# Norm statistics of a two-block fp32 transformer kernel: plain sums and row broadcasts by transposes and a row sum, in place of fp32 products with ones and with the identity

## The chip, the cores and the metric

The kernel runs on one NeuronCore of a Trainium2 chip. The metric is the time of one execution on the device in microseconds (us); the lower, the better. The kernel before takes 892.62 us, the median of 3 runs (891.92 to 893.26).

## The reference

Two transformer blocks run one after the other on one sequence of 256 tokens with 1024 features, all in fp32. The first block has a sliding-window attention layer with sinks and a block attention layer. The second has two layers, each a hybrid mixer (dilated attention beside a chunked state-space scan) and a gated feed-forward. What the change touches are the norms:

```python
def rmsnorm(x, g):
    y = x * lax.rsqrt(jnp.mean(x * x, axis=-1, keepdims=True) + NORM_EPS)
    return y * g

def first_block(x, ...):
    h = x
    for i in range(DEPTH):                 # 2 layers: phases a, ao and b, bo
        hn = rmsnorm(h, norm_g[i])
        ...                                # q, k, v, z; rope; attention
        h = h + (o * jax.nn.silu(z)) @ w_out[i]
    return rmsnorm(h, final_g)

def second_block(x, ...):
    for layer in range(DEPTH):             # phases m0, mo0, f0, fo0 and m1, mo1, f1, fo1
        h = h + hybrid_mixer(rmsnorm_2(h, norm_mix[layer]), ...)
        h = h + swiglu(rmsnorm_2(h, norm_ffn[layer]), ...)
    return rmsnorm_2(h, final_norm)
```

Inside the hybrid mixer the scan's output is normalised once more, in two groups of 512 features. That makes six norms over 1024 features on the way (phases a, b, m0, f0, m1, f1; the one of m0 has two sums, because the final norm of the first block and the first norm of the second block are taken together), four group norms, and the last norm of all.

## The kernel before

Features lie on the 128 partitions and tokens along the free axis, so that a tile is 128 features by 256 tokens. Every dense product is made of three f32r products (high part by high, high by low, low by high), which are matmuls of 128x128 weights with 128x256 moving columns. ScalarE (ACT) rounds an operand or a weight tile to its high part (names `hi`, `r`, `x`), VectorE (DVE) makes the low part (`lo`). Weights come in by DMA on SyncE's queue (L1451).

The whole program is written out in advance, in the order of an expected timeline. The class `Build` keeps a clock for each engine. `cost` (L219) holds the expected time of an instruction and `account` (L247) adds it to the clocks. The planner `run_plan` (L471) goes through a fixed list of dense products and issues one slot of them as soon as its operands are expected. Everything else (norms, rotary embedding, softmax, scan) runs in side chains, Python generators whose next step `step_sides` (L298) issues once its operands are expected to be there. So the side work stands between dense products, at places that depend on every expected time. A side chain takes one of the 8 PSUM banks by `take` (L282) and returns it by `give` (L287). There are limits by kind: 2 banks at most for kind "tr", which the norms share with the transposes of the attention and of the scan. On each engine the instructions then run strictly in the order of the program.

All instructions pass through one helper, so the profile puts them all on line L78, and they are told apart by tile names: the phase, two underscores, the tile. `a__sm` is the tile `sm` of phase a; matmul outputs are called `p`.

The norm (`norm`, L650) runs as a side chain with these steps:

- `squares` (L891) adds up x squared over the feature tiles, and `columns` (L579) adds the two halves on VectorE into `sm` [128 features, 256 tokens].
- TensorE multiplies each half of `sm` with a column of ones, in native fp32. The result is a column of sums, tokens on partitions, in PSUM: `p<-ones,sm`, 128x1 twice.
- VectorE divides and adds epsilon (`s<-p`, 128x2), and GpSimd (POOL) takes the power -1/2.
- `rows` (L622) turns the column into rows on all partitions: a native fp32 product of the column, broadcast along the free axis, with the identity, twice (`p<-cst,s`; `cst` holds the identity). VectorE copies the row out of PSUM (`row`, and `rowh`, its half).

The dense products of a phase start before its norm is done: the norm's scale per token is applied when a finished unit leaves PSUM (`q`, `k`, `v` tables, `zh`, `u`, `up`). A phase has one norm, and m0 calls `columns` with two sums and `rows` twice: in all 11 pairs of products with ones and 11 pairs with the identity. `scan_out` (L1240) calls `norm` for the group norms in phases mo0 and mo1. The last norm of the program and the sums of the scan's time steps do not use these functions.

Two chains of other work matter below. The attention issues, for a pair of heads, the score products (`p<-rope,rope`, TensorE), a masked minimum on VectorE (`sm<-p,cst`, shown as CUSTOM_DVE), the exponential on ScalarE (`pe`), the scaling on VectorE (`pe<-pe,s`), three transposes per head on TensorE (`p<-cst,pe`), a copy (`pt`) and the product with the values (`p<-pt,vk`). The last attention outputs of a phase are the last operands of the output projection (phases ao, bo, mo0, mo1). In the scan, ScalarE makes decay masks (`m`), and TensorE multiplies them (`p<-m,xg`).

Of the kernel before, what the change touches and what calls it, by code (L numbers as in the profile page):

```python
# [16 lines left out]
OP = mybir.AluOpType  # L17
# [11 lines left out]
# column offsets of the packed per-feature vectors  # L29
# [14 lines left out]
# column offsets of the constants (they depend on shapes alone)  # L44
# [20 lines left out]
class Engine:  # L65
    """Passes instructions on and notes how long they are expected to take."""
# [24 lines left out]
class Chain:  # L91
    """A generator of steps; a step is issued once what it waits for is expected to be there."""
# [7 lines left out]
class Timed(dict):  # L100
    """Results with the times at which they are expected."""
# [11 lines left out]
class Build:  # L113
    """Emits the program in the order of an expected timeline: the dense products keep the tensor engine
    busy, and the steps of the side chains are issued between them as their operands come up."""
# [84 lines left out]
    def drop(self, n=1):  # L200
        """n pages have had their last use issued."""
        self.live -= n
# [16 lines left out]
    def cost(self, eng, op, args, kw):  # L219
# [21 lines left out]
        if eng == "POOL":  # L241
            return 650.0
        if op in ("tensor_copy", "tensor_scalar") and not psum:
            return 68.0 + 0.52 * n + 93.0 * cols
# [20 lines left out]
    def calm(self, ns):  # L265
        """Hold new side work back while the vector or scalar engine has much to do."""
        while max(self.clk["DVE"], self.clk["ACT"]) > self.clk["PE"] + ns:
            yield "poll"

    def bank_at(self, kind):  # L270
        """When a PSUM bank can be had, or None."""
        if self.used[kind] >= self.CAPS[kind] or not self.banks:
            return None
        if kind == "mm" and self.used["mm"] >= 3 and len(self.banks) < 4:
            return None
        return min(self.banks)
# [21 lines left out]
    def step_sides(self):  # L298
        """Issue every step that is due; the least time at which another will be."""
# [25 lines left out]
    def seg(self, key, w, unit, k0, k1, kt, xkey, done, mode="T", page=False):  # L325
        """Plan the contraction tiles k0..k1 of one unit of 256 columns."""
# [7 lines left out]
    def feed_dma(self):  # L334
        """Load the next segment."""
# [18 lines left out]
    def feed(self):  # L354
        """Issue loads and splits ahead of the products."""
# [3 lines left out]
        while self.cast_i < self.dma_i and self.cast_slot < self.slot + self.LEAD:  # L359
# [15 lines left out]
            if s["mode"] == "dt":  # L375
                # both parts of the 16 columns side by side
                both = hi[:, :, 0:32]
                raw, hi, lo = raw[:, :, 0:16], both[:, :, 0:16], both[:, :, 16:32]
            else:
                lo = self.fp.tile([P, n, S], F32R, tag="f", name=self.name("lo"))  # L380
# [20 lines left out]
    def slot_ready(self):  # L401
        """When the next slot of the dense products can start, if that is known."""
# [121 lines left out]
    def rotary_tables(self):  # L524
        """Tables of the second block from the positions."""
# [39 lines left out]
    def split_scaled(self, h, off, u, key, g=None):  # L565
        """Parts of h * g for one unit of two feature tiles."""
# [12 lines left out]
    def columns(self, accs, ns):  # L579
        """Sums of squares [128, 2, 256] -> 1/rms per token in columns [128, 2]; a second sum is of the  # L580
        values once normalised by the first."""
# [9 lines left out]
        ps = self.bank("tr", (P, 4))  # L591
        for j, sm in enumerate(sms):
            for b in range(2):
                nc.tensor.matmul(ps[:, 2 * j + b:2 * j + b + 1], sm[:, b * P:(b + 1) * P], self.ones[:, 0:1],
                                 start=True, stop=True, skip_group_check=True)
            self.drop()
        yield 1
        cols = []
# [6 lines left out]
        self.give("tr")  # L605
# [16 lines left out]
    def rows(self, rc, key, half=True):  # L622
        """Columns per token -> [128, 256] rows on every partition (and their half)."""
# [3 lines left out]
        for b in range(2):  # L627
            nc.tensor.matmul(pr[:, b * P:(b + 1) * P], rc[:, b:b + 1].to_broadcast([P, P]), self.ident,
                             start=True, stop=True)
# [16 lines left out]
    def keep(self, key, n=1):  # L646
        """n pages that live as long as the phase."""
# [12 lines left out]
    def spare(self, ns):  # L660
        """Whether the scalar engine is free ns earlier than the vector engine."""
# [3 lines left out]
    def scaled(self, out, src, scale):  # L665
        """out = src * scale (a column per partition) on the engine that is free first."""
# [20 lines left out]
    def rope(self, ps, nt, tab, mask, key, give=True):  # L687
        """nt tiles of PSUM [128, nt, 256] rotated."""
# [18 lines left out]
    def v_tokens(self, ps, row, key):  # L707
        """[128 channels, 256 tokens] -> [128 tokens, 2 blocks, 128 channels]"""
# [33 lines left out]
    def gate_unit(self, key, u):  # L742
        """silu of the normalised columns."""
# [15 lines left out]
    def scores(self, q, k, mask, sinks, key, last):  # L759
        """Scores of two heads; they take different rows of the array, side by side."""  # L760
# [16 lines left out]
    def head(self, sc, mask, sink, key):  # L777
        """Probabilities of one head, keys on partitions:
        [keys 0..127 x queries 0..255 | keys 128..255 x queries 128..255]"""
# [38 lines left out]
    def attention(self, key, units, kname, vcols, mask, sinks, finish):  # L818
        """Heads in pairs of tiles; finish(u, po) takes the two tiles of a unit from PSUM."""
# [55 lines left out]
    def out_unit(self, key, u, hkey, hnext, scale):  # L875
        """h += o @ w for one unit, with the parts of the next norm's input."""
# [36 lines left out]
    def plan_out(self, key, w, kt, cuts, hkey, hnext, scale):  # L913
        """The contraction tiles that come up late are left to later parts of the units."""
# [7 lines left out]
    def plan_in(self, lst):  # L922
        """Units of 8 contraction tiles; the first two leave the tiles that come last to the end."""
# [142 lines left out]
    def dt_unit(self, l):  # L1066
        """dt and a = dt * a_neg, [128 tokens, 2 blocks, 16 heads] each."""
        def done(ps):
# [49 lines left out]
            # cumulated a per block of tokens (negated), and from a token to the end of the first block  # L1118
# [17 lines left out]
            # the sums per head on the partitions, as three parts of bf16 that add up to them  # L1136
# [20 lines left out]
    def cb_chain(self, l):  # L1157
        """B C^T with the earlier tokens on partitions, per group: first block x all tokens, second x second."""
# [16 lines left out]
    def decay(self, l, u, c):  # L1175
        """M^T = exp(sum of a from a token to a later one) * B C^T of four heads, earlier tokens on partitions;
        c is the block of the later tokens."""
# [34 lines left out]
    def state_inputs(self, l, u):  # L1212
        """xs of four heads with tokens on partitions times dt; xs itself times d_skip."""
# [26 lines left out]
    def scan_out(self, l, u):  # L1240
        """Outputs of four heads, gated, and the group norm once its two units are there."""
# [49 lines left out]
    def plan_m(self, l):  # L1291
# [36 lines left out]
        def residual():  # L1328
            # the first block's output: h * final_g / rms
# [48 lines left out]
    def last_unit(self, t0, n):  # L1378
        """The last residual for feature tiles t0..t0+n-1: sums of squares per token, and the tiles times the
        final gain with tokens on partitions; with the last of them the result."""  # L1380
# [68 lines left out]
    def load(self, out, src, n):  # L1449
        """A load of n bytes per partition; its tile's results come up when it has landed."""  # L1450
# [87 lines left out]
def _units(w, cols):  # L1538
    """[K, N] -> [units, 128, K / 128, 256], columns in the given order."""
# [5 lines left out]
def _feat(v):  # L1545
    """[..., n * 128] -> [128, rows * n]"""
# [107 lines left out]
```

## Time and profile before

| what | us |
|---|---|
| median of 3 runs | 892.62 |
| span of the profiled execution | 889.3 |
| TensorE (PE) busy | 872.1 (98%) |
| VectorE (DVE) busy | 702.4 (79%) |
| ScalarE (ACT) busy | 527.0 (59%) |
| GpSimd (POOL) busy | 12.8 (1%) |
| DMA, mean rate | 160 GB/s |

The profile is one execution, whose span runs from its first to its last recorded instruction. The median lies 3.3 us above that span. The span is cut into stretches by the phases: the chain that ended last gives phase b's dense products from 108.14 us, bo 180.45, m0 210.39, mo0 some 316, f0 356.31, fo0 483.91, m1 547.27, mo1 649.48, f1 687.33 us. A row of the timeline has a start and a duration; matmuls overlap in the pipeline, so that what a matmul costs is read from the start of the next one and not from its duration. A native fp32 product is recorded as two instructions, so that a pair shows as "x4".

### The profile page before, as it was taken

The numbers are of one execution on the slowest core, as the hardware profiler recorded it, in microseconds if no ns is written. First come the engines' busy times: TensorE is split into PE (matmuls) and PEld (weight loads), VectorE is DVE, ScalarE is ACT, GpSimd is POOL, SyncE is SP. The second block draws the span as 40 slices with busy tenths as digits, with TensorE's granted clock in tenths as the row PEclk, the third lists the DMA queues.
The fourth block names the chain that finished last, engine by engine and source line by source line (L and its number), as shares of the span: only waits on it lengthen the run. The fifth ranks groups of instructions, "written<-read, shape, count | busy, mean of one in ns | idle before, by whom it ended". The sixth has DMA issues, their size and how long they took to land.

```text
span 889.3 us, 18454 instructions
## 1 busy us (share of the span) xinstructions
PE 872.1 (98%) x7318; PEld 841.8 (95%) x7318; DVE 702.4 (79%) x1542; ACT 527.0 (59%) x1217; POOL 12.8 (1%) x30
## 2 busy tenths in 40 slices
PE   6999999999999999999999999999999999999996
PEld 6987999889998889999999999999999999999996
DVE  5999889998899998998667547888988898667331
ACT  6378753677778875665345446668656675444321
POOL 0000000000000000000000000000000000000000
PEclk9999999999999999999999999999999999999998
DMA  8522773035542146767444637520047687545501
GB/s 298 205 86 72 236 262 125 26 114 179 186 152 98 37 131 208 278 241 280 153 157 146 220 132 245 185 73 25 1 134 225 244 282 258 186 132 171 173 1 48
DMA packets 30390, 142.39 MB, mean 160 GB/s; under 512 B 5344, under 2 KB 6880, under 8 KB 18400
## 3 DMA queue, kind: packets, MB, share of 16 engines
q1 hardware_dynamic: 30304, 141.22, 46.8%
q8 instruction: 57, 0.93, 0.4%
q14 instruction: 29, 0.24, 0.1%
HBM read 140.15 MB, written 1.05 MB: 159 GB/s over the span
## 4 chain that ended last, share of the span: by engine, by line
PE 68%; issue 21%; DVE 5%; ACT 3%; DMA 2%; SPq 1%; POOL 0%; POOLq 0%; DVEq 0%
PE m__p L78 21%; PE f__p L78 15%; PE mo__p L78 9%; PE b__p L78 8%; PE fo__p L78 7%; PE bo__p L78 3%; PE ao__p L78 3%; PE a__p L78 1%; DVE a__lo L78 1%; DVE a__sm L78 1%; ACT m__m L78 1%; DMA cst<-cst 1%; DMA fo__raw<-wa 1%; DVE a__pe L78 1%; DVE a__rope L78 1%
## 5 line engine op out<-in xcount | busy, mean ns | idle before, releaser
L78 PE MATMUL f__p<-mo__x,f__hi 128*128 128x256 f32 x808 | 147.4, 283 | 0.0
L78 PEld LDWEIGHTS f__p<-mo__x,f__hi 128*128 128x128 f32 x808 | 126.0, 192 | 0.0
L78 DVE TENSOR_TENSOR f__lo<-f__raw,f__hi 128x512 fp32r<-128x512 f32 x184 | 119.6, 685 | 3.0 <-ACT f__hi L78 2.1
L78 PE MATMUL f__p<-mo__x,f__lo 128*128 128x256 f32 x404 | 114.3, 283 | 0.0
L78 ACT ACTIVATE f__hi<-f__raw 128x512 fp32r<-128x512 f32 x183 | 100.1, 617 | 10.6 <-DMA f__raw<-wg 6.7
L78 PE MATMUL f__p<-f__x,f__hi 128*128 128x256 f32 x528 | 97.0, 283 | 0.0
L78 PEld LDWEIGHTS f__p<-f__x,f__hi 128*128 128x128 f32 x528 | 82.4, 192 | 0.0
L78 PEld LDWEIGHTS f__p<-mo__x,f__lo 128*128 128x128 f32 x404 | 77.6, 192 | 0.0
L78 PE MATMUL f__p<-f__x,f__lo 128*128 128x256 f32 x264 | 74.7, 283 | 0.0
L78 PE MATMUL fo__p<-f__r,fo__hi 128*128 128x256 f32 x400 | 72.7, 284 | 0.0
L78 PEld LDWEIGHTS fo__p<-f__r,fo__hi 128*128 128x128 f32 x400 | 62.4, 192 | 0.0
L78 DVE TENSOR_TENSOR m__lo<-m__raw,m__hi 128x512 fp32r<-128x512 f32 x74 | 50.2, 687 | 12.1 <-ACT m__hi L78 11.5
L78 PE MATMUL fo__p<-f__r,fo__lo 128*128 128x256 f32 x200 | 56.6, 283 | 0.0
L78 PE MATMUL m__p<-bo__x,m__hi 128*128 128x256 f32 (+1 forms) x292 | 54.3, 287 | 0.5 <-ACT m__m L78 0.5
L78 PE MATMUL a__p<-fo__x,a__hi 128*128 128x256 f32 x280 | 52.8, 289 | 1.0 <-ACT a__hi L78 1.0
L78 PE MATMUL mo__p<-mo__r,mo__hi 128*128 128x256 f32 x288 | 52.5, 284 | 0.0
L78 PEld LDWEIGHTS f__p<-f__x,f__lo 128*128 128x128 f32 x264 | 50.7, 192 | 0.0
L78 PEld LDWEIGHTS m__p<-bo__x,m__hi 128*128 128x128 f32 (+1 forms) x292 | 44.9, 188 | 2.4 <-issue 1.3
L78 ACT ACTIVATE m__hi<-m__raw 128x512 fp32r<-128x512 f32 x69 | 41.9, 633 | 7.3 <-DMA m__raw<-w 7.3
L78 PEld LDWEIGHTS a__p<-fo__x,a__hi 128*128 128x128 f32 x280 | 43.9, 193 | 2.3 <-ACT a__hi L78 1.5
L78 ACT ACTIVATE f__r<-f__up 128x512 fp32r<-128x512 f32 x20 | 12.6, 632 | 55.8 <-DVE f__up L78 55.6
L78 PEld LDWEIGHTS mo__p<-mo__r,mo__hi 128*128 128x128 f32 x288 | 44.9, 192 | 0.2 <-issue 0.2
(534 smaller groups left out, 2432.1 us busy)
## 6 DMA issues: line engine op xcount, KB each, us to landing
f__raw<-wu SPq DMA_DIRECT2D x20, 1024.0 KB, 4.9
f__raw<-wg SPq DMA_DIRECT2D x18, 1024.0 KB, 5.0
m__raw<-w SPq DMA_DIRECT2D x17, 1024.0 KB, 5.0
f__raw<-wd SPq DMA_DIRECT2D x10, 1024.0 KB, 4.9
b__raw<-wb SPq DMA_DIRECT2D x7, 1024.0 KB, 6.2
mo__raw<-wo SPq DMA_DIRECT2D x12, 512.0 KB, 4.0
fo__raw<-wd SPq DMA_DIRECT2D x6, 1024.0 KB, 5.1
fo__raw<-w SPq DMA_DIRECT2D x5, 1024.0 KB, 5.9
```

Of the source, the lines that this page charges most:

```text
L78: return fn(*args, **kw)
```

## The change

In `columns`, the two products with ones become two transposes of `sm` (128x128 each) into a PSUM tile of 128x2x128, and VectorE sums each transposed half along the free axis (`tensor_reduce`) into a small SBUF tile. The PSUM bank is given back after the reduce. The scalar step then reads SBUF. In `rows`, the two products with the identity become two transposes of the broadcast column. `cost` gets a line for the reduce. All other lines of the diff are comments and docstrings.

```diff
@@ -240,6 +240,8 @@ def cost
             return 650.0
+        if op == "tensor_reduce":
+            return 130.0 + 1.042 * args[1].shape[1] * args[1].shape[2]
         if op in ("tensor_copy", "tensor_scalar") and not psum:
@@ -588,13 +590,17 @@ def columns
         yield 1
         yield from self.take("tr")
-        ps = self.bank("tr", (P, 4))
+        tr = self.bank("tr", (P, len(sms), 2, P))
         for j, sm in enumerate(sms):
             for b in range(2):
-                nc.tensor.matmul(ps[:, 2 * j + b:2 * j + b + 1], sm[:, b * P:(b + 1) * P], self.ones[:, 0:1],
-                                 start=True, stop=True, skip_group_check=True)
+                nc.tensor.transpose(tr[:, j, b, :], sm[:, b * P:(b + 1) * P], self.ident)
             self.drop()
         yield 1
+
+        ps = self.small(4)
+        for j in range(len(sms)):
+            nc.vector.tensor_reduce(ps[:, 2 * j:2 * j + 2], tr[:, j, :, :], mybir.AxisListType.X, OP.add)
+        self.give("tr")
         cols = []
@@ -602,7 +608,6 @@
         t = self.small()
         nc.vector.tensor_scalar(t, ps[:, 0:2], 1.0 / ns, EPS, op0=OP.mult, op1=OP.add)
-        self.give("tr")
         rc = self.small()
@@ -620,13 +625,12 @@ def rows
         pr = self.bank("tr", (P, S))
         for b in range(2):
-            nc.tensor.matmul(pr[:, b * P:(b + 1) * P], rc[:, b:b + 1].to_broadcast([P, P]), self.ident,
-                             start=True, stop=True)
+            nc.tensor.transpose(pr[:, b * P:(b + 1) * P], rc[:, b:b + 1].to_broadcast([P, P]), self.ident)
         yield 1
```

The expected times change, so the planner also puts other work at other places from phase a on. Three places follow.

The norm of phase b on VectorE. The rows run from the tile of sums `sm` to the scalar step `s`. Before:

```order
L78 TENSOR_TENSOR b__sm_1714<-b__sq_1680 128x256
L78 TENSOR_TENSOR b__lo_1731<-ao__raw_1601,b__hi_1730 128x512
L78 TENSOR_TENSOR b__lo_1741<-ao__raw_1601,b__hi_1740 128x512
L78 TENSOR_TENSOR b__lo_1754<-ao__raw_1601,b__hi_1753 128x512
L78 TENSOR_TENSOR b__lo_1758<-ao__raw_1601,b__hi_1757 128x512
L78 TENSOR_SCALAR b__s_1761<-b__p_1744 128x2
```

After:

```order
L78 TENSOR_TENSOR b__sm_1718<-b__sq_1695 128x256
L78 TENSOR_TENSOR b__lo_1739<-ao__raw_1597,b__hi_1738 128x512
L78 TENSOR_TENSOR b__lo_1749<-ao__raw_1597,b__hi_1748 128x512
L78 TENSOR_TENSOR b__lo_1762<-ao__raw_1597,b__hi_1761 128x512
L78 TENSOR_REDUCE b__s_1765<-b__p_1752 128x2
L78 TENSOR_SCALAR b__s_1767<-b__s_1765 128x2
```

One reduce is added per sum; its listed shape is that of its output. The scalar step stays behind it.

The last attention heads of phase a on TensorE, in phase ao. The `pe` tiles are those of one head each, `pt` and `vk` belong to the product with the values, and rows with `hi` or `lo` are dense products. Before, from the transposes of the last head but one on:

```order
L78 MATMUL ao__p_1360<-cst,ao__pe_1241 128x128 x3
L78 MATMUL ao__p_1364<-ao__pt_1301,a__vk_633 64x256
L78 MATMUL ao__p_1364<-ao__pt_1343,a__vk_633 64x256
L78 MATMUL ao__p_1364<-ao__pt_1301,a__vk_633 64x128
L78 MATMUL ao__p_1364<-ao__pt_1343,a__vk_633 64x128
...
L78 MATMUL ao__p_1392<-cst,ao__pe_1259 128x128 x3
...
L78 MATMUL ao__p_1364<-ao__pt_1369,a__vk_633 64x256
```

After, the last four heads:

```order
L78 MATMUL ao__p_1298<-cst,ao__pe_1179 128x128 x3
L78 MATMUL ao__p_1302<-cst,ao__pe_1207 128x128 x3
L78 MATMUL ao__p_1315<-cst,ao__pe_1230 128x128 x3
...
L78 MATMUL ao__p_1334<-cst,ao__pe_1243 128x128 x3
L78 MATMUL ao__p_1331<-ao__pt_1313,a__vk_654 64x256
L78 MATMUL ao__p_1331<-ao__pt_1319,a__vk_654 64x256
L78 MATMUL ao__p_1331<-ao__pt_1313,a__vk_654 64x128
L78 MATMUL ao__p_1331<-ao__pt_1319,a__vk_654 64x128
...
L78 MATMUL ao__p_1331<-ao__pt_1332,a__vk_654 64x256
```

The first three of these four heads now follow each other with no dense product between them, where 30 dense products stood among the same heads before. The gap to the last head is 6 dense products (12 before). Ahead of the last transposes TensorE has 456 dense products of phases a and ao (492 before), and behind the last product with values 162 dense products of ao come without a break (126 before).

The end of the attention of m0 on TensorE, where phase mo0 begins: the score products of the last pair of heads (`rope,rope`). Before, they are followed by dense products of phase m0:

```order
L78 MATMUL m__p_4547<-m__cs_4047,sel 128x128
L78 MATMUL m__p_4565<-m__rope_3726,m__rope_4170 128x128
L78 MATMUL m__p_4566<-m__rope_3726,m__rope_4170 128x128
L78 MATMUL m__p_4565<-m__rope_3726,m__rope_4170 128x256
L78 MATMUL m__p_4566<-m__rope_3726,m__rope_4170 128x256
L78 MATMUL m__p_4470<-bo__x_3072,m__hi_4428 128x256
```

After:

```order
L78 MATMUL mo__p_4751<-m__r_4417,mo__lo_4694 128x256
L78 MATMUL mo__p_4773<-m__rope_3731,m__rope_4163 128x128
L78 MATMUL mo__p_4774<-m__rope_3731,m__rope_4163 128x128
L78 MATMUL mo__p_4773<-m__rope_3731,m__rope_4163 128x256
L78 MATMUL mo__p_4774<-m__rope_3731,m__rope_4163 128x256
...
L78 MATMUL mo__p_4786<-cst,mo__sm_4749 128x128 x2
L78 MATMUL mo__p_4811<-cst,mo__xs_4770 128x128 x4
L78 MATMUL mo__p_4829<-cst,mo__s_4800 128x128 x2
...
L78 MATMUL mo__p_4851<-cst,mo__pe_4791 128x128 x3
L78 MATMUL mo__p_4860<-cst,mo__pe_4803 128x128 x3
L78 MATMUL mo__p_4772<-mo__pt_4858,m__vk_3869 64x256
```

The score products now stand behind the 48 dense products of mo0 that need no late operand. Before, 36 dense products of m0 and 48 of mo0 stood between them and the last product with values; now none does, only small products of the other head pair, the group norm and the scan (`m,xg`, 12 rows).

## Rows read from the trace of the kernel before

**Rows 1.** The page, busy time and share of the span by engine.

```profile
PE 872.1 (98%) x7318; PEld 841.8 (95%) x7318; DVE 702.4 (79%) x1542; ACT 527.0 (59%) x1217; POOL 12.8 (1%) x30
```

**Rows 2.** The chain that ended last: start us, duration us, what; phases b and f0.

```profile
108.14 72.31 PE b__p L78 x606
...
356.31 127.60 PE f__p L78 x1064
```

**Rows 3.** Windows: start:end, length, busy PE, PEld, DVE, ACT, POOL, clock, DMA.

```profile
66.00:82.00 16.00, 15.15 (x127) 11.96 (x125) 15.51 (x63) 14.65 (x51) 0.00 (x0) 1.00 0.21 67
...
283.00:322.00 39.00, 37.67 (x341) 32.15 (x339) 36.58 (x88) 34.41 (x108) 0.00 (x0) 1.00 0.19 55
...
356.00:484.00 128.00, 128.00 (x1070) 128.00 (x1069) 100.27 (x166) 67.41 (x125) 1.07 (x1) 1.00 0.60 211
```

**Rows 4.** Timeline of PE, phase b: start us, duration us, instruction, [idle <-releaser].

```profile
115.89 0.51 PE L78 MATMUL b__p<-ones,b__sm 128*128 128x1 f32 x4
116.26 0.48 PE L78 MATMUL b__p<-b__x,b__hi 128*128 128x256 f32 x2
```

**Rows 5.** Timeline of PE, phase m0, the product with the identity.

```profile
228.83 0.60 PE L78 MATMUL m__p<-cst,m__s 128*128 128x128 f32 x4
229.19 0.48 PE L78 MATMUL m__p<-bo__x,m__hi 128*128 128x256 f32 x2
```

**Rows 6.** Timeline of PE, phase a, two transposes and the next product.

```profile
43.80 0.38 PE L78 MATMUL a__p<-cst,a__vt 128*128 128x128 f32 x2
43.94 0.48 PE L78 MATMUL a__p<-fo__x,a__hi 128*128 128x256 f32 x2
```

**Rows 7.** Groups by form, PE: transposes (count, busy us, mean ns, idle before).

```profile
L78 PE MATMUL m__p<-cst,m__xs 128*128 128x128 f32 x24 | 3.8, 279 | 0.0
```

**Rows 8.** Groups by form, DVE: instructions near to the new row sum.

```profile
L78 DVE CUSTOM_DVE_ANT_0 m__sm<-m__p,cst 128x256 f32<-128x256 f32 x16 | 6.7, 420 | 0.0
...
L78 DVE COPY m__row<-m__p 128x256 f32<-128x256 f32 x4 | 1.7, 421 | 0.9 <-PE m__p L78 0.9
...
L78 DVE TENSOR_SCALAR m__s<-m__p 128x2 f32<-128x2 f32 x4 | 0.5, 155 | 0.7 <-PE m__p L78 0.7
```

**Rows 9.** Timeline of DVE and PE around the end of phase a's attention.

```profile
33.92 0.01 DVE L78 LOAD_MASK_SELECT a__rot<-a__p  x1 [0.89 <-PE a__p L78]
...
77.50 0.69 DVE L78 TENSOR_TENSOR a__lo<-a__raw,a__hi 128x512 fp32r<-128x512 f32 x1
78.10 0.69 DVE L78 TENSOR_TENSOR a__o<-a__p,a__gt 128x512 f32<-128x512 f32 x1
...
80.37 0.55 PE L78 MATMUL ao__p<-cst,a__pe 128*128 128x128 f32 x3 [0.59 <-DVE a__s L78]
...
89.35 0.55 DVE L78 TENSOR_SCALAR ao__pe<-ao__pe,ao__s 128x128 f32<-128x128 f32 x2
...
90.83 0.49 PE L78 MATMUL ao__p<-cst,ao__pe 128*128 128x128 f32 x3
...
91.96 0.87 PE L78 MATMUL ao__p<-ao__pt,a__vk 128*64 128x256 f32 x8
92.76 0.50 PE L78 MATMUL ao__p<-ao__r,ao__hi 128*128 128x256 f32 x2
```

**Rows 10.** Timeline of DVE, PE and ACT around the end of phase m0's attention.

```profile
295.30 0.69 DVE L78 TENSOR_TENSOR m__lo<-m__raw,m__hi 128x512 fp32r<-128x512 f32 x1 [2.04 <-ACT m__hi L78]
...
303.82 0.93 PE L78 MATMUL m__p<-m__rope,m__rope 64*128 64x128 f32 x8
...
307.11 0.28 DVE L78 CUSTOM_DVE_ANT_0 m__sm<-m__p,cst 128x128 f32<-128x128 f32 x1
...
321.01 1.23 PE L78 MATMUL mo__p<-mo__pt,m__vk 128*64 128x256 f32 x8
...
322.87 1.75 ACT L78 ACTIVATE mo__xg<-mo__p,m__t 128x64 f32<-128x64 f32 x8
...
326.07 0.50 PE L78 MATMUL mo__p<-mo__r,mo__hi 128*128 128x256 f32 x2
```

## Prediction, made before the changed kernel had run

> **What bounds the kernel now.** I read the busy times first: TensorE is busy 98% of the span, VectorE 79%, ScalarE 59% [rows 1]. The chain of waits says where that holds: from phase b on it is one engine's dense products in long pieces, 72.31 us in b, 127.60 us in f0, without a wait [rows 2]. So wherever TensorE has its operands, the kernel gets faster by exactly the work taken from it. The windows then show the two places that are not like this. In 66 to 82 us VectorE works 15.51 of 16.00 us and TensorE only 15.15; in 283 to 322 us VectorE has 36.58 and ScalarE 34.41 of 39.00 us, and TensorE lacks 1.3 us [rows 3]. Both are the ends of an attention, where its last outputs are needed for the output projection. In f0, for comparison, VectorE has 28 us to spare in 128 [rows 3]. So the forecast has three terms: TensorE work removed, VectorE work added, and what the new order does to the two ends of attention.
>
> **TensorE, columns.** A pair of products with ones starts at 115.89 and the next dense product at 116.26: it costs 0.37 us, not the 0.51 of its row, because the pipeline overlaps [rows 4]. The new pair of transposes is an operation that the kernel already has: the pair at 43.80 is followed at 43.94, so it costs 0.14 us [rows 6]. Saved: 0.23 us for each of 11 pairs, 2.5 us.
>
> **TensorE, rows.** A pair with the identity costs 229.19 - 228.83 = 0.36 us [rows 5], and becomes a pair of transposes at 0.14 [rows 6]. The moving operand is a column read with stride 0, which no transpose of the trace has; the products with the identity read the same column in this way already. Saved 0.22 x 11 = 2.4 us. Bounds: if such a transpose cost what the product cost, nothing; cheaper than 0.14 nothing suggests. Together TensorE loses **5.0 us** of work, 0.45 per norm.
>
> On transposes the rows show a difference between duration and price: 24 transposes of the scan last 279 ns each on average [rows 7], but two of them delay the dense stream by 0.14 us [rows 6]. The Trainium skill, page "TensorE: Matmul & The Clock Gate", section "Part 4: PE-mode transpose", gives about 275 ns for a 128x128 transpose within a kernel. The trace agrees as to the duration. Were that figure the price in the stream, the sum below would come out some 9 us higher, an estimate from the page's figure; this is the third rival.
>
> **VectorE.** Each of the 11 sums gets a row sum of 2x128 values from PSUM. No row sum of this kind is in the trace. Nearest are the copy of 128x256 out of PSUM at 421 ns and the masked minimum over 128x256, which also reads PSUM and reduces, at 420 ns [rows 8]. Below, a 128x2 step takes 155 ns [rows 8]; above, I allow twice the copy, 0.84 us. I take 0.42, 4.6 us in all. The scalar step now reads SBUF and stays at its 155 ns. In b, f0, m1 and f1 the cover is VectorE's own spare time [rows 3], and nothing on TensorE waits for a norm soon: the dense products do not use it before their unit is finished. There the reduce costs nothing. If that cover were gone, each would cost its 0.42. The scalar step, GpSimd's power and the row come at most 0.4 us later, less the 0.2 that TensorE is sooner. The PSUM bank is held through the reduce; that delays only other transposes of kind "tr", in the planner's order.
>
> **The order, phase a.** Here the saving cannot be taken off the end, because VectorE is the limit. The last scaled probabilities end on VectorE at 89.35 + 0.55 = 89.90, and the transposes that take them start at 90.83, so TensorE had 0.93 us of slack there [rows 9]. In the new order VectorE has two `lo` and one `o` less ahead of that point, each 78.10 - 77.50 = 0.60 us, and the reduce more: 1.4 us sooner. One `lo` more stands before the shuffle at 33.92 that waits 0.89 us for TensorE, so up to 0.9 us of that wait is filled with work [rows 9]. Together the probabilities end at 87.6 at the earliest. TensorE, however, has 36 dense products fewer ahead (0.12 us each, 4.3 us), a product with the values fewer (92.76 - 91.96 = 0.80) and the norm's 0.45: it would be at those transposes at 90.83 - 5.6 = 85.2. It waits 2.4 us or, as the heads before it share VectorE, a little more. The missing dense products stand behind it, so the wait is not made good. b then starts at 108.14 - 0.45 + 2.5 = 110.2, **2.1 us later** instead of 0.45 earlier. Bounds: no wait at all (-0.45), or the shuffle's wait stays and VectorE comes 0.9 later (+3.0). The present waits there, 0.59 us and its like [rows 9], go in either case; they are part of the same limit.
>
> **The order, b to mo0.** b and m0 save 0.45 and 0.9 (m0 has two sums). The last score products of m0 ran at 303.82, VectorE took the first of their minima at 307.11 [rows 10], and 84 dense products (10 us) covered the rest of that chain. In the new order VectorE has 30 instructions, some 15 us, more ahead of these minima. Its wait of 2.04 us at 295.30 [rows 10] and the smaller ones behind can be filled, so they come near 320. TensorE has nothing dense left then. From the minima to the next dense product I count: two heads' minima 1.2 us (two parts each, 0.28 and 0.42 [rows 8, 10]), exponential and scaling some 2.3, scaling to product with the values 91.96 - 89.35 = 2.6 [rows 9], from there to dense work 326.07 - 321.01 = 5.06 before, of which 1.75 was ScalarE's scan step [rows 10], so 3.3: 9.4 in all with nothing else in the way, some 8.7 if steps of the two heads overlap. Dense work resumes near 328.7 against 326.07 [rows 10], with the same 240 dense products to follow as before. Less the group norm's 0.45, f0 starts **2.1 us later** than 356.31 [rows 2]. This contains phase a's loss: mo0 by itself costs 1.3 us beyond a's 2.1 carried on, less the savings of b and m0 (1.35). Bounds: 0 to 3 us more for this chain, as ScalarE may be free or busy.
>
> **Sum.** f0, m1, the two group norms of mo1 and f1 save 5 x 0.45 = 2.25 us, with TensorE the only limit. +2.1 - 2.25 = -0.15, rounded to -0.2 us, on the profiled span of 889.3; the median of the runs is 3.3 us above that span, so 892.62 - 0.2 = **892.4 us**.
>
> **Rivals.**
>
> 1. *The saving comes through.* If VectorE and ScalarE run the new order without the waits above, everything removed from TensorE shows: 892.62 - 5.0 = 887.6. For it: no dense product depends on a norm; VectorE gains 1.4 us at the end of phase a. Against: 162 dense products now stand behind the last attention product of a, and none before that of m0. If only one of the two places waits, it is near 890 (887.6 plus 2.5 for a, or plus some 2 for mo0).
> 2. *Slower: the tail of m0's attention becomes the bound.* In 283 to 322 VectorE has only 2.4 us of idle time and ScalarE 4.6 [rows 3]. If the minima come not at 320 but, with phase a's full 3.0 us, two reduces of 0.84 and none of VectorE's waits filled, at 322 or 323, each microsecond is a microsecond of TensorE standing still, since no dense product is left to cover it. That gives 893.5 to 896. It decides from the minima at 321.5 on.
> 3. *Transposes at their duration.* If 44 transposes stopped the dense stream for 279 ns each [rows 7], they would cost 12.3 us, against 11 x 0.73 = 8.0 for what goes: 4.3 us slower instead of 5.0 faster, 892.4 + 9.3 = 901.7. Rows 6 speak against it. The page named above has its figure near to this duration.
>
> That the change doesn't do what it says is hardly possible: 22 products and 22 products are replaced one for one in the order.
>
> **Chances.** Both places wait as worked out, 890.8 to 894.4: 0.42. Only one of them waits, or both less: 0.24, below 890.8. Neither waits: 0.12, near 887.6. The slower tail: 0.20, and transposes at their duration: 0.02. About 0.2% (1.8 us) is what a measurement of this kernel can tell from no change, so the bounds are 890.8 and 894.4: faster 0.36, same 0.42, slower 0.22. The range is 888.0 to 895.8: it takes in most of the cases with one wait and of the slower tail, and leaves out most of rival 1's end and rival 3.
>
> **What would show it.** Right: in the profile after, pairs of `ones,sm` are gone, transposes of `sm` and of `s` are followed by dense work 0.14 us after their start; row sums last near 0.42 us; b starts near 110 and waits of TensorE for VectorE or ScalarE stand in 84 to 89 us; dense work of mo0 has a hole of several microseconds before 329; from f0 to the end everything is 2.25 us shorter. Wrong: b starts at 107.7, or f0 at 353.6, which would be rival 1; f0 after 360, rival 2; a gap of 0.28 us or more behind each transpose, rival 3; or a new wait in f0 to f1, where I expect none.

## The result and the profile after

The changed kernel takes **901.81 us** (median of 4 runs, 899.85 to 903.35) against 892.27 us (891.5 to 893.26) for the kernel before: a ratio of 1.011, 95% interval 1.0098 to 1.0122. It is about 9.5 us slower. The forecast was 892.4 us, with a range of 888.0 to 895.8.

The page of the changed kernel, busy time and share of the span, with the granted clock in 40 slices, against [rows 1]:

```profile
span 901.2 us, 18377 instructions
...
PE 876.7 (97%) x7274; PEld 842.2 (93%) x7274; DVE 706.7 (78%) x1552; ACT 527.6 (59%) x1216; POOL 12.7 (1%) x30
...
PEclk9998999999999989999999999999999999999999
```

VectorE has 4.3 us more to do, near the 4.6 reckoned for the row sums. TensorE has fewer instructions and yet more busy time than before (872.1), and in two slices the granted clock is below 9 tenths.

First the new operations, in the timeline of TensorE in phases b and m0 (start, duration, instruction), against [rows 4, 5]:

```profile
123.28 0.38 PE L78 MATMUL b__p<-cst,b__sm 128*128 128x128 f32 x2
123.41 0.48 PE L78 MATMUL b__p<-b__hi,ao__x 128*128 128x256 f32 x2
...
235.53 0.38 PE L78 MATMUL m__p<-cst,m__s 128*128 128x128 f32 x2
235.66 0.48 PE L78 MATMUL m__p<-m__x,m__hi 128*128 128x256 f32 x2
```

and in the groups by form of VectorE (count, busy us, mean ns, idle before), against [rows 8]:

```profile
L78 DVE TENSOR_REDUCE m__s<-m__p 128x2 f32<-128x256 f32 x4 | 1.6, 422 | 1.6 <-PE m__p L78 1.6
```

Both kinds of transposes delay the dense stream by 0.13 us a pair, also the one that reads a column with stride 0; a row sum lasts 422 ns. The prices of the forecast (0.14 us, 0.42 us) were right.

So the time went elsewhere. The waits of TensorE in the changed kernel (who waited, for whom: us in total, times, longest):

```profile
PE mo__p L78 <- DVE mo__s L78: 2.2, 1, 2.2
PE mo__p L78 <- DVE mo__r L78: 1.6, 2, 1.3
PE ao__p L78 <- DVE a__pe L78: 1.4, 1, 1.4
PE mo__p L78 <- ACT mo__r L78: 1.3, 1, 1.3
PE mo__p L78 <- DVE mo__sm L78: 1.0, 1, 1.0
...
PE ao__p L78 <- DVE ao__pe L78: 0.8, 1, 0.8
```

All are at ends of an attention or a scan. The forecast had looked for two such holes; the 1.3 of `mo__r` is in a third, behind m1. The windows show the other part: two stretches of the kernel before, then six of the changed kernel. Columns: stretch, length, busy PE, PEld, DVE, ACT, POOL, granted clock, DMA share, GB/s.

```profile
84.00:88.00 4.00, 4.00 (x36) 4.00 (x35) 3.86 (x16) 3.89 (x13) 0.00 (x0) 1.00 0.45 131
88.00:92.00 4.00, 4.00 (x36) 3.38 (x35) 3.93 (x10) 2.80 (x6) 0.00 (x0) 1.00 0.36 131
...
80.00:84.00 4.00, 2.54 (x22) 1.42 (x20) 3.93 (x18) 4.00 (x16) 0.00 (x0) 1.00 0.23 54
84.00:88.00 4.00, 2.83 (x11) 2.18 (x13) 3.79 (x20) 3.33 (x15) 0.00 (x0) 0.62 0.20 79
88.00:92.00 4.00, 4.00 (x22) 3.30 (x19) 2.36 (x10) 1.73 (x4) 0.00 (x0) 0.52 0.02 4
...
322.00:326.00 4.00, 2.28 (x20) 1.22 (x19) 3.96 (x8) 1.15 (x2) 0.00 (x0) 1.00 0.79 248
326.00:330.00 4.00, 2.16 (x10) 1.44 (x12) 3.97 (x17) 2.38 (x9) 0.69 (x1) 0.67 0.46 134
330.00:334.00 4.00, 4.00 (x31) 3.33 (x28) 3.93 (x13) 0.58 (x2) 0.00 (x0) 0.50 0.00 0
```

In the changed kernel VectorE is full in most of these stretches and TensorE is not. After each hole TensorE goes on at a granted clock near one half (1.2 instead of 2.4 GHz), in 88 to 92 us with 22 instructions in 4 us against 36 before. The forecast had nothing on the clock.

### The profile page after: what moved, and what is told of

Read it like the earlier page. It is cut to its first block, busy times and chain, and to the rows that moved or that the text cites. A ratio compares the mean times of both kernels' runs of the same rounds, so it can differ in the third digit from the quotient of the medians.

```text
span 901.2 us, 18377 instructions
## 1 busy us (share of the span) xinstructions
PE 876.7 (97%) x7274; PEld 842.2 (93%) x7274; DVE 706.7 (78%) x1552; ACT 527.6 (59%) x1216; POOL 12.7 (1%) x30
## 3 DMA queue, kind: packets, MB, share of 16 engines
HBM read 140.15 MB, written 1.05 MB: 157 GB/s over the span
## 4 chain that ended last, share of the span: by engine, by line
PE 69%; issue 21%; DVE 5%; DMA 3%; ACT 1%; SPq 1%; POOL 0%; POOLq 0%; DVEq 0%
PE m__p L78 22%; PE f__p L78 15%; PE b__p L78 8%; PE fo__p L78 7%; PE mo__p L78 6%; PE a__p L78 4%; PE bo__p L78 3%; PE ao__p L78 3%; DMA mo__raw<-wo 1%; DMA fo__raw<-wa 1%; DMA cst<-cst 1%; DVE mo__lo L78 1%; SPq L1455 1%; DVE a__pe L78 1%; DVE a__sm L78 0%
## 5 line engine op out<-in xcount | busy, mean ns | idle before, releaser
L78 PE MATMUL f__p<-f__x,f__hi 128*128 128x256 f32 x672 | 123.0, 283 | 0.0
L78 DVE TENSOR_TENSOR f__lo<-f__raw,f__hi 128x512 fp32r<-128x512 f32 x180 | 117.0, 685 | 0.8
L78 PE MATMUL f__p<-mo__x,f__hi 128*128 128x256 f32 x640 | 117.0, 283 | 0.0
L78 PEld LDWEIGHTS f__p<-f__x,f__hi 128*128 128x128 f32 x672 | 104.8, 192 | 0.0
L78 PEld LDWEIGHTS f__p<-mo__x,f__hi 128*128 128x128 f32 x640 | 99.8, 192 | 0.0
L78 PE MATMUL f__p<-f__x,f__lo 128*128 128x256 f32 x336 | 95.1, 283 | 0.0
L78 PE MATMUL f__p<-mo__x,f__lo 128*128 128x256 f32 x320 | 90.6, 283 | 0.0
L78 PEld LDWEIGHTS f__p<-f__x,f__lo 128*128 128x128 f32 x336 | 64.5, 192 | 0.0
L78 PEld LDWEIGHTS f__p<-mo__x,f__lo 128*128 128x128 f32 x320 | 61.4, 192 | 0.0
L78 PE MATMUL mo__p<-mo__r,mo__hi 128*128 128x256 f32 x288 | 54.4, 290 | 3.0 <-DVE mo__r L78 1.6
```

The source lines that it names most:

```text
L78: return fn(*args, **kw)
```

## Where the time went, stage by stage

The starts of the first dense product of a phase cut the profiled execution into stages. Each figure is the difference of two starts in the timeline of one kernel. The first column begins at the transposes or products of phase a's sums, so that the first loads, which differ by up to 1 us from one execution to the next, are left out.

| kernel (profile) | sums of a to b | b to f0 | f0 to m1 | m1 to f1 | f1 to the end |
|---|---|---|---|---|---|
| before | 83.92 | 248.18 | 190.96 | 140.05 | 202.14 |
| changed | 89.61 | 253.44 | 190.49 | 140.99 | 201.64 |
| changed, a second time | 88.68 | 253.25 | 190.49 | 141.05 | 201.59 |
| e1, new operations, old order | 83.95 | 246.88 | 190.48 | 138.66 | 201.62 |
| e2, old operations, new order | 89.06 | 252.87 | 190.96 | 142.10 | 202.09 |
| e4, old prices in a and ao | 83.97 | 254.66 | 190.67 | 140.99 | 201.63 |
| e5, old prices from b on | 88.68 | 250.87 | 190.50 | 138.66 | 201.59 |
| e7, rows alone, own order | 83.84 | 254.75 | 190.72 | 143.15 | 201.85 |
| e8, changed with fillers | 88.06 | 252.63 | 191.26 | 140.64 | 201.59 |

From f0 to m1 and from f1 to the end, where TensorE alone is the limit, the changed kernel gains 0.47 and 0.50 us, one norm each, as forecast. It loses 5.7 us in phase a, 5.3 us between b and f0, and 0.9 us between m1 and f1. Each row is one execution, and some lie away from the median of their kernel's runs: e7 3.1 us above it, e4 1.7 and the changed kernel 1.5 above, e5 1.5 below. In its second profile the changed kernel loses 4.8 us in phase a and 5.1 between b and f0.

## The experiments

The **theory** after the result: the operations are cheap as reckoned, and the loss is the planner's new order, which leaves the ends of attention without cover; part of it is the half clock behind the holes. The **rival**: the operations themselves cost the time in some way that their rows don't show.

**e1: new operations in the old order.** The planner is told the old prices (`fix` overrides `cost`; `real` passes an instruction on without counting it). Every engine's instructions then stand as before, but for the replaced ones and the row sums; by tile names, the traces of the two kernels show the same order on all four engines. Lines left out are marked by dots, here and below.

```diff
@@ columns
+                self.fix = 220.0
                 nc.tensor.transpose(tr[:, j, b, :], sm[:, b * P:(b + 1) * P], self.ident)
+                self.fix = None
...
-            nc.vector.tensor_reduce(...)
-        self.give("tr")
+            nc.vector.real.tensor_reduce(...)
+        self.fix = 130.0 + 1.042 * 2
...
+        self.fix = None
+        self.give("tr")
@@ rows
+            self.fix = 128 / 2.4 * 4 * 1.02
             nc.tensor.transpose(pr[:, b * P:(b + 1) * P], rc[:, b:b + 1].to_broadcast([P, P]), self.ident)
+            self.fix = None
```

> All new operations (transposes, row sums), but the planner is told the old prices, so that every engine runs in the order of the kernel before; the 11 row sums are put in without being counted. Theory (the operations are cheap, the loss is the order): TensorE has 5.0 us less to do and no new hole, so 892.3 - 5.0 = 887.3 us, 886.5 to 888.5; phase b starts 0.45 us sooner, every norm after it gives another 0.45. Rival (the new operations themselves cost the time): near the changed kernel, 900 us or more.

Measured: 888.35 us against 891.8 on the same chip, ratio 0.9962 (0.995 to 0.9975); a second time 887.97 against 891.78, ratio 0.9956 (0.9943 to 0.9968). The operations make the kernel faster; the rival is out. The gain is 3.4 to 3.8 us and not 5.0. By the table, b to f0 gives 1.3 instead of the 2.25 of its five pairs of each kind, and phase a nothing instead of 0.45. Between b and f0 some 0.4 us are longer waits of TensorE at the end of m0's attention (0.8 us for `mo__pt` instead of 0.6, and 0.2 for `mo__sm`); the rest is open. In phase a the cause is a wait of 0.45 us that was forecast to hurt nobody: the row sum delays GpSimd's power, and the row product, which stands at a fixed place in TensorE's order, now waits for it. In the timeline of e1:

```profile
25.13 0.42 DVE L608 TENSOR_REDUCE a__s<-a__p 128x2 f32<-128x256 f32 x1 [0.34 <-PE a__p L78]
...
25.91 1.00 POOL L78 TENSOR_TENSOR a__s<-a__s,mhalf 128x2 f32<-128x2 f32 x1 [25.04 <-DVE a__s L78]
...
26.97 0.43 PE L78 MATMUL a__p<-cst,a__s 128*128 128x128 f32 x2 [0.45 <-POOL a__s L78]
```

This kernel beats both others.

**e2: old operations in the new order.** The mirror image: the kernel before, with the planner told the new prices, and the row sum put on VectorE's clock without being issued.

```diff
@@ columns
+                self.fix = 110.0
                 nc.tensor.matmul(ps[:, ...], sm[:, ...], self.ones[:, 0:1], ...)
+                self.fix = None
...
+        self.fix = 130.0 + 1.042 * 256
+        for j in range(len(sms)):
+            self.account("DVE", "tensor_reduce", (), {})
+        self.give("tr")
+        self.fix = 68.0 + 0.52 * 2
...
```

The products of `rows` get the new price, 110.0, in the same way. By tile names the traces show the order of the changed kernel, without its row sums.

> All old operations (products with ones and with the identity, no row sum), but the planner is told the new prices, so that every engine runs in the order of the changed kernel. Theory: the holes of the changed kernel stay and TensorE has 5 us more to do, part of it hidden in the holes: 901.8 + 3 to 5 = 904.5 to 907 us. Rival (the operations): back at 892 us.

Measured: 904.32 us, ratio 1.0141 (1.0127 to 1.0154), 0.2 us below the range expected. The four corners agree, each taken against the kernel before on its own chip: 12.5 us slower here (904.32 - 891.8), 9.3 to 9.5 slower for the changed kernel, 3.4 to 3.8 faster for e1. So the new order costs 12.5 us with the old operations and 12.7 to 13.3 with the new ones, and the new operations save 3.4 to 3.8 us in the old order and 3.0 to 3.2 in the new one. The holes are there without any row sum, so VectorE's new work is not their cause either.

**e4 and e5: old prices in one part of the program.** In e4 the price overrides hold in phases a and ao, in e5 everywhere else (`self.fix = 220.0 if self.phase in ("a", "ao") else None`, and likewise for the others).

> The changed kernel, but the planner has the old prices in phases a and ao and the new ones from b on. The end of phase a's attention is then ordered as before; the end of m0's attention has its score products behind the dense products of mo0, as in the changed kernel. Theory: only the hole in mo0 and the half clock behind it remain: f0's start relative to b's start is 253.4 us as in the changed kernel (248.2 before), the whole 893.5 to 895.5 us. If the hole in a alone were the loss: 887.5 us. If neither: 901 us.

> The changed kernel, but the planner has the new prices in phases a and ao and the old ones from b on. The end of phase a's attention is ordered as in the changed kernel; the end of m0's attention is again mixed with dense products. Theory: only the hole in a and the half clock behind it remain: b starts at 113 to 115 us, f0 starts some 247 us after b (248.2 before, less the saved work), the whole 893 to 895 us. If the hole in mo0 alone were the loss: 887.5 us.

Measured: e4 896.61 us (ratio 1.0046, 1.0031 to 1.0062), e5 898.1 us (ratio 1.0069, 1.0055 to 1.0083). The losses are local: e4 has phase a of e1 (83.97) and the loss between b and f0 (254.66), e5 has phase a of the changed kernel (88.68). They are 1.1 and 3.1 us above the ranges expected; the runs of e4 lie between 894.54 and 898.32, and the profiled one is the longest. In e4 mo0 is a little worse than in the changed kernel. In e5 the orders of b to mo0 are new as well, and b to f0 takes 4 us longer than in e1; one wait of 1.7 us in bo is among them. The two also part in m1 to f1: with the order of the changed kernel 140.99, with the old one 138.66. That is a third place, which costs 2.3 us.

**e7: rows alone.** Only `rows` is changed, in the planner's own order.

```diff
@@ rows
-            nc.tensor.matmul(pr[:, b * P:(b + 1) * P], rc[:, b:b + 1].to_broadcast([P, P]), self.ident,
-                             start=True, stop=True)
+            nc.tensor.transpose(pr[:, b * P:(b + 1) * P], rc[:, b:b + 1].to_broadcast([P, P]), self.ident)
```

> Only the rows by transposes, the sums by products with ones as before; the planner's own prices and order. The operations would give 2.4 us: 889.4. In its order the end of phase a's attention is still mixed with dense products (b starts at 107.5 to 109 us), but at the end of m0's attention the last score products again stand behind all but a few dense products. Theory (the order decides): a hole and half clock in mo0, f0 starts 252 to 255 us after b, the whole 895 to 898 us. Rival (the prices decide): 889.4 us.

Measured: 900.5 us, ratio 1.0095 (1.0068 to 1.0122), above the 895 to 898 expected: phase a as before (83.84), b to f0 254.75, and m1 to f1 even 143.15, in the longest of its runs. Half of the change, with another order, loses nearly as much. Here, what a change of price does to the plan is not in proportion to the change.

**e3, e3a, e3m and e8: the holes filled.** To separate the waits from the half clock, products of the identity with itself, which nobody reads, are put in front of the waiting instructions. `FA` and `FM` hold how many go where, 15 in ao and 32 in mo0; two of the seven places are shown:

```diff
+    def fill(self, out, n):
+        for _ in range(n):
+            self.nc.tensor.real.matmul(out, self.ident, self.ident, start=True, stop=True, skip_group_check=True)
@@ head
+        if key[0] == "a":
+            self.fill(tr[:, 0:P], FA.get(self.heads, 0))
@@ state_inputs
+        if self.phase == "mo0":
+            self.fill(tr[:, 0, 0, :], FM.get("xs", 0))
```

> The changed kernel in its own order, plus products of the identity with itself on TensorE that nobody reads, put in front of the waiting instructions at the two ends of attention (15 in ao, 32 in mo0; each about 0.18 us, written to a PSUM bank that the following instruction overwrites, 9 of them to a bank already read). They fill the waits and carry no data. Theory (a hole costs twice, once as a wait and once because TensorE works at half clock behind it): the granted clock stays at 1.00 in 80 to 92 and 322 to 344 us and the kernel gets faster by doing more: 901.8 - 4 to 6 = 896 to 898 us. Rival (the waits alone are the loss): no change, 901.8, or slower by what the fillers exceed the waits, up to 8 us.

> The same with the 15 fillers in ao alone. Theory: half clock in 84 to 92 us goes, half clock in mo0 stays: 901.8 - 2 to 3 = 899 to 900 us. Rival: 901.8 or more.

> The same with the 32 fillers in mo0 alone. Theory: half clock in 84 to 92 us stays, half clock in 324 to 344 us goes: 901.8 - 2 to 4 = 898 to 900 us. Rival: 901.8 or more.

Measured: 902.75, 901.03 and 904.0 us; ratios to the kernel before 1.012 (1.0089 to 1.0151), 1.0091 (1.0064 to 1.0117), 1.0128 (1.0107 to 1.0149). None reaches the range expected (896 to 898, 899 to 900, 898 to 900). The a part did its work on the clock: in e3a it is 1.00 in all of 80 to 96 us, and phase a takes 88.05. The mo0 part was a bad experiment: the fillers were written to the bank of the next transposes, and that bank was what these had waited for. The timeline of e3 shows ten fillers (20 records) waiting themselves and then standing in the chain:

```profile
325.76 3.99 PE L589 MATMUL mo__p<-cst 128*128 128x128 f32 x20 [2.31 <-DVE mo__s L82]
329.59 0.60 PE L82 MATMUL mo__p<-cst,mo__xs 128*128 128x128 f32 x4
```

In e8 the fillers of mo0 go to the half of the attention's bank that the last product with the values overwrites, and there are 44 of them instead of 32. One of the places:

```diff
@@ state_inputs
         if self.phase == "mo0":
-            self.fill(tr[:, 0, 0, :], FM.get("xs", 0))
+            self.fill(self.res["po", "m0", 1][:, 1, 0:P], FM.get("xs", 0))
```

> As the run with fillers at both ends, but the 33 fillers in front of the waiting instructions of mo0 go to the half of the attention's PSUM bank that the last product with the values overwrites, so that they wait for nobody (before, most of them stood behind a wait of 2.3 us for a bank and lengthened the chain); 11 more as before in a bank already read. Theory (half clock behind the holes costs time of its own): granted clock 1.00 in 84 to 92 and 322 to 344 us; from the start of b to the start of f0 250 to 251.5 us instead of 253.4, from phase a's sums to the start of b 88.0 instead of 89.6; the whole 3 to 5 us below the changed kernel run beside it. Rival (the waits alone): no gain on the changed kernel.

> The changed kernel once more, beside the run with fillers on the same chip: 901 to 903 us by both theories, with the granted clock at half in 84 to 92 and in 326 to 341 us.

Measured: 900.33 us (ratio 1.009, 1.0076 to 1.0103) beside 901.4 for the changed kernel (1.010, 1.0086 to 1.0115). The windows of e8:

```profile
84.00:88.00 4.00, 3.28 (x26) 2.43 (x25) 3.76 (x19) 2.92 (x13) 0.00 (x0) 1.00 0.14 54
88.00:92.00 4.00, 4.00 (x37) 3.52 (x36) 3.40 (x10) 3.40 (x8) 0.00 (x0) 1.00 0.00 0
...
326.00:330.00 4.00, 4.00 (x48) 3.71 (x47) 3.93 (x18) 1.50 (x8) 0.69 (x1) 1.00 0.11 45
330.00:334.00 4.00, 4.00 (x36) 3.56 (x37) 3.37 (x7) 1.72 (x4) 0.00 (x0) 1.00 0.00 0
```

The clock now stays at 1.00, and the time falls by 1.1 us, with intervals that overlap, not by the 3 to 5 expected. In the changed kernel's second profile the clock was not at half throughout, as expected, but 0.85 and 0.73 in 84 to 92 us and between 0.50 and 0.83 in 326 to 342.

By stages, phase a gains 0.6 to 1.6 us in e8 and b to f0 0.6 to 0.8, while f0 to m1 loses 0.8: there TensorE waits 0.58 us for a sum of f0's norm, as it does not in the changed kernel. The gain between b and f0 is a difference of two parts. These are the first minimum and the dense work behind the hole in e8:

```profile
324.94 0.28 DVE L82 CUSTOM_DVE_ANT_0 mo__sm<-mo__p,cst 128x128 f32<-128x128 f32 x1
...
336.03 0.48 PE L82 MATMUL mo__p<-mo__r,mo__hi 128*128 128x256 f32 x2
```

The minimum comes 212.26 us after b's start, as in the changed kernel (212.25). From there to the dense work it takes 11.1 us instead of 9.8, which the fillers add, and from there to f0 29.3 instead of 31.4. Of these 2.1 us, 0.34 are a wait of the changed kernel, so the half clock behind the hole costs some 1.8 us here. With phase a that makes some 2.4 to 3.3 us for the half clock, and most of the loss stays with the clock at full speed: the waits are the main part. What the half clock costs within the chain, between the minima and the dense work, is not shown, since the fillers lengthen it.

**e9: each row sum twice**, in the old order, to price it (`tensor_reduce` issued a second time).

> New operations in the order of the kernel before, with each row sum done twice: VectorE gets 11 x 0.42 = 4.6 us more, none of it counted by the planner. It prices the row sum. Theory: in b, f0, m1 and f1 VectorE hides it; in a the row product waits 0.45 us more for GpSimd; in a's and mo0's ends, where VectorE is full, up to 0.4 to 0.8 us each: 0.5 to 1.6 us above the run with one row sum beside it. Rival (VectorE is the limit all along): 4.6 us above. If the row sum is hidden everywhere: no difference.

> New operations in the order of the kernel before, once more, beside the run with each row sum done twice: 888 to 889 us; phase b starts 83.9 us after phase a's sums, f0 starts 246.9 us after b.

Measured: 889.49 us beside 887.97, 1.5 us more for 4.6 us of VectorE work. In the profiles, phase a takes 0.44 us more, b to f0 0.37, m1 to f1 0.40, and from f0 to m1 and from f1 to the end nothing. So VectorE hides two thirds of the row sums' time. Where it shows, the row product waits for GpSimd's power: 0.91 us instead of 0.45 in phase a, and two waits that e1 does not have, 0.5 us in mo0 and 0.2 in m1.

## Why the prediction was wrong

The term that failed is the order. Forecast were 2.1 us lost in phase a, nothing between b and f0, and 2.25 us saved from f0 on. The runs show 4.8 to 5.7 us lost in phase a, 5.1 to 5.3 between b and f0, and nothing saved from f0 on, since 0.9 to 1.0 us lost between m1 and f1 use up the gain of the other two stages.

- **The prices of the operations** were right (0.13 for 0.14 us, 422 for 421 ns), and so were the stages with TensorE alone as the limit. That the result is near the 901.7 us of the third rival is chance: its mechanism, transposes that hold up the stream for their duration, is refuted by the 0.13 us. The Trainium skill, page "TensorE: Matmul & The Clock Gate", section "Part 4: PE-mode transpose", gives about 275 ns for a 128x128 transpose in a kernel, and the type it names is bf16. The norms' fp32 transposes here last 270 to 272 ns at the full clock, so that the figure again agrees as a duration, and by the 0.13 us not as a price.
- **The order, phase a** named the place and was mis-sized: 2.1 us later was forecast, 4.8 to 5.7 came. Two steps failed. First, VectorE did not come 2.3 us sooner but 1.2. Its work up to the last probabilities fell by 1.45 us (61.59 against 63.04), as reckoned, but its idle time rose from 2.8 to 3.1 us, where 0.9 was to go. The forecast let VectorE fill its wait at the shuffle, and took for granted that it would go on without new waits. In the changed kernel it waits for ScalarE in the middle of its full stretch:

```profile
61.08 0.16 DVE L78 TENSOR_TENSOR a__s<-a__s,a__s 128x2 f32<-128x2 f32 x1 [1.43 <-ACT a__s L78]
```

Second, the last head was taken as the one that TensorE waits for. The waits begin five heads earlier. Behind them the clock is at half, and so are the nine transposes of the three heads before the last. VectorE ends the last head at 89.70, but its transposes start at 92.18:

```profile
83.35 0.61 PE L78 MATMUL ao__p<-cst,a__pe 128*128 128x128 f32 x3 [1.42 <-DVE a__pe L78]
84.79 0.95 PE L78 MATMUL ao__p<-cst,ao__pe 128*128 128x128 f32 x3 [0.83 <-DVE ao__pe L78]
...
89.15 0.55 DVE L78 TENSOR_SCALAR ao__pe<-ao__pe,ao__s 128x128 f32<-128x128 f32 x2
89.18 2.18 PE L78 MATMUL ao__p<-cst,ao__pe 128*128 128x128 f32 x9
...
92.18 0.49 PE L78 MATMUL ao__p<-cst,ao__pe 128*128 128x128 f32 x3
```

That makes 2.1 + 1.1 + 2.5 = 5.7 us. With the clock held up (e8) the last transposes start 0.9 us behind VectorE instead of 2.5, and phase a takes 4.1 us longer than before; the rest, 0.6 to 1.6 us, is the half clock, of which the forecast said nothing.

- **The order, b to mo0** had the right place and mechanism too: the score products behind the last dense products, the minima late on VectorE. Forecast was that b to f0 would take as long as before (f0 and b both 2.1 us later); it took 5.1 to 5.3 us longer. The minima came 212.25 us after b's start instead of 199.14 before, 13.1 us later, where 10.7 had been reckoned (320 with b at 110.2). Between b's start and the minima VectorE has 15.2 us more work (196.18 against 180.97) and only 2.1 us less idle time (16.1 against 18.2), where 320 took some 4 us off (307.11 + 2.1 + 15 is 324.2), more than the 2.4 us that VectorE was idle in 283 to 322 us [rows 3]. From the minima to the dense work it took 9.8 us instead of 8.7, and from there to f0 31.4 instead of 29.6 (30.1 before, less a norm), with half clock in both. That is 2.4 + 1.1 + 1.8 = 5.3 us:

```profile
322.14 0.93 PE L78 MATMUL mo__p<-m__rope,m__rope 64*128 64x128 f32 x8
...
326.89 0.28 DVE L78 CUSTOM_DVE_ANT_0 mo__sm<-mo__p,cst 128x128 f32<-128x128 f32 x1
...
327.57 1.11 PE L78 MATMUL mo__p<-cst,mo__xs 128*128 128x128 f32 x4 [2.25 <-DVE mo__s L78]
...
336.67 0.38 PE L78 MATMUL mo__p<-mo__r,mo__hi 128*128 128x256 f32 x1 [1.35 <-ACT mo__r L78]
```

This is the second rival, the slower tail, by more than it allowed. It was given 0.20.

- **"f0 to f1, where I expect none"** was wrong. Between m1 and f1 the new order puts an operand of the projection behind ScalarE's roundings of late weights, TensorE waits 1.28 us for it, and the 1.4 us of three norms become a loss of 0.9. The forecast read no row of mo1's order. Of the 2.3 us over the old order this leaves 1.0, by which TensorE is busy longer (139.71 us against 138.65 in e1); the reason is open.

```profile
688.06 0.39 PE L78 MATMUL mo__p<-mo__r,mo__hi 128*128 128x256 f32 x1 [1.28 <-DVE mo__r L78]
```

- **The base** was right to 0.4 us (892.27 here, 892.62 there). The time of a run is 2.15 us above its span here (903.35 against 901.2) and not 3.3, so the profiled execution of before, with 889.3, lies some 0.8 us below the median, and that of the changed kernel lies 1.5 above. That is why the stages of the table add up to 10.9 us and the medians differ by 9.5.

Not settled is how the 1.2 to 1.6 us split by which e1 falls short of 5.0, beyond the waits named, and the exact share of the half clock, since fillers of exactly the length of each wait were not tried.

## What to carry to other kernels

Where a planner sets the order from expected times, a new price makes a new program: keep the old order by keeping the old prices, measure the operations in it, and take a new order only if it is faster by itself. Here that turns 9.5 us of loss into 3.4 to 3.8 us of gain with the same operations. When an order is judged without a run, follow every chain that ends in a late operand: which instruction is the first to wait, what new waits the engine behind it gets, and whether dense work is left to cover it. Here savings spread over the whole program did not pay for three uncovered chains.

## What was unexpected of the hardware

Behind holes in TensorE's work the granted clock fell to about one half: 0.62 and 0.52 in 84 to 92 us, after waits of 1.42 and 0.83 us, between which and up to 85.39 us TensorE ran six transposes and nothing else, and 0.67 and 0.50 in 326 to 334 us, after waits of 1.05 and 2.25 us. It was at 1.00 again in 92 to 96 and in 342 to 346 us. In the kernel before, a wait of 0.59 us at the same end of phase a [rows 9] left it at 1.00. The same program with the same waits of 1.42 and 0.83 us had 0.85 and 0.73 in 84 to 92 us in its second profile, and phase a was 0.9 us shorter. Work that nobody needs kept the clock at 1.00 in e8, where it waited for nobody; in e3, where it waited itself, the clock fell to 0.63 in 326 to 330 us. e8 gained 1.1 us in all, while the fillers lengthened one chain by 1.3 us and f0 to m1 lost 0.8.
